# One rotary product in each attention step, output additions behind the keys' low parts, a gate operand in halves, and a shorter look-ahead for the first feed-forward pairs

## The chip, the cores and the metric

The kernel runs on one core of a Trainium2 chip. The metric is the time of one execution in microseconds on the device, lower being better. Five engines take part: TensorE (PE in the profile, with its weight loads as PEld), VectorE (DVE), ScalarE (ACT), GpSimd (POOL) and SyncE (SP), which issues DMAs. Each engine runs its own list of instructions in the order in which the program wrote them, and waits on semaphores for the others.

## The reference

One encoder block on 1024 tokens of width 1024, in float32. What is computed, cut to its core:

```python
h = layer_norm(x, ln0_g, ln0_b)
proj = h @ w_in[l] + b_in[l]
qa, ka, va, qb, kb, vb, ga, gb = jnp.split(proj, IN_SPLITS, axis=-1)
qb = partial_rotary(qb.reshape(B, S, SWA_Q_HEADS, HEAD_DIM), pos)
kb = partial_rotary(kb.reshape(B, S, SWA_KV_HEADS, HEAD_DIM), pos)
y_na = neighbourhood_attention(qa, ka, va, na_rpb[l]) @ w_branch_na[l]
y_swa = windowed_gqa_with_sink(qb, kb, vb, swa_sink[l]) @ w_branch_swa[l]
mixed = jax.nn.sigmoid(ga) * y_na + jax.nn.sigmoid(gb) * y_swa
h = layer_norm(DEEPNORM_ALPHA * h + mixed @ w_out[l] + b_out[l], ln1_g[l], ln1_b[l])
u = jnp.square(jax.nn.relu(h @ w_ff1[l] + b_ff1[l]))
h = layer_norm(DEEPNORM_ALPHA * h + u @ w_ff2[l] + b_ff2[l], ln2_g[l], ln2_b[l])
```

There are eight heads of windowed attention (SWA; 128 tokens to each side, a sink logit per head in the softmax's denominator, two key/value heads) and eight of two-dimensional neighbourhood attention (NA, with a bias table). The rotary turn acts on 16 of the 64 dimensions of SWA's queries and keys.

## The kernel before

**Precision.** Most products are made in three passes from a high and a low part of each operand (high·high, high·low, low·high). So each operand costs a rounding copy, mostly on ACT, and a subtraction, mostly on DVE. `hT` holds the normalised input, transposed; `whi` and `wlo` are the two parts of a weight block, and L278 is the matmul of the projections.

**Stages.** First the layer norm and the first gate products, until about 50 us. Then projections, until about 90. Then 64 attention steps, until about 450: sixteen heads with four steps each, SWA's in steps 0 to 31 and NA's in 32 to 63. Next are the gates (a Strassen scheme over blocks, operands S1 to S3, L851 its matmul, until 545), the branches, the output projection with its layer norm (to 735), the first feed-forward product (FF1, to 1040) and the second (to the end).

**One attention step.** `steps(s)` (L751) writes the parts of different steps in this order:

- `part_a2(s+1)`: DVE adds the sink's share to the sums (L563, SWA alone), takes their reciprocal (L564) and scales the two blocks of exponentials (L567, twice);
- `part_a(s+2)`: PE makes two blocks of scores (L530 and L531). DVE reads each from PSUM, adds the bias and takes the maxima (L533), and then makes the negated maxima (one small instruction, L539 in SWA, L537 in NA);
- a slice of the work that `pump` hands out: the projections of later heads;
- `part_b(s)`: PE transposes the scaled blocks (L588), ACT rounds them (L591), and DVE makes their low parts (L594). `part_e(s+2)`, the exponentials on ACT (L551), is written in the middle of it;
- `flush(False)`, another slice of `pump`, `part_c(s-1)` (PE, L624: the product with the values; in every second step ACT copies one half of it out, L630, and DVE adds the other, L631), `flush`, and the rest of `pump`.

Below, a step is numbered by the count n of L564 on DVE, from 0 at 94.31 us.

**The list `later`.** `defer(0, f, 8, g, ...)` puts functions on a list. Each `flush` runs the entries whose count has come to zero, oldest first, and a number ahead of a function is the count of flushes till it runs. What is deferred is so written behind what is on the list already. Through it go the evacuations of projections:

- `rope` (L385) for SWA's queries and keys: ACT copies the projection out (`qf`, L393), DVE shuffles it (`qs`, L398), POOL makes two products and their sum (L399, L400, L401: 128x512 each), and ACT and DVE make high and low parts (L437, L442). Ten such turns are made, five of them beside attention steps. `rt` holds the cosines and sines.
- `proj_na_qk` (L340) for NA: ACT writes three high parts (L348 to L350), and after `D_NA` flushes DVE makes the low parts `q` and `kl` (L353, L355, L357).
- `turn_v` (L320): ACT's copy and DVE's subtraction for the values `vv` (L326, L327).

**Gates.** `form_hi("S3", g2)` is one ACT copy of a 128x2048 operand into a part of `hT`, `form_lo` one DVE subtraction of that size (L891). `g_sums`, `g_hi` and `g_lo` make a gate's weight operands (L821, L837, L841).

**FF1.** `seq` lists pairs (p, i): block p of the hidden units, product i of seven in a Strassen step. The loop at L1702 runs them: `ff1_mm` on PE (L1313) and `after1` behind it, which evacuates a bank (`act_fn`: DVE L1399 to `usl`). Ahead of each, `prep_to(k)` runs `tick` until k ticks are done. A tick makes the low part of a pair's weights (L1497), the high part of the next pair's (ACT, L1493) and the sums of the pair behind it (L1467, L1482), and asks for later blocks by DMA (`raw`). The larger k is, the more such work is written ahead of the evacuation that follows.

Of the kernel before, what the change touches and what calls it, by code (L numbers as in the profile page):

```python
# [15 lines left out]
P = 128  # L16
# [39 lines left out]
RS = 3, 3.5, 4.5, 5.5  # L56
HI_AT = -1
HI_ACT = (2, 3, 4, 5), ()
ST0=2
# [23 lines left out]
def encoder_block(ctx, tc, x, w_in, w_br, w_out, w_ff1, w_ff2, par, rows, rpbp,  # L83
# [4 lines left out]
    def b32(ap):  # L88
        return ap.bitcast(F32)
# [292 lines left out]

    n_rope = [0]

    def rope(ps, bias, half, then, late=D_ROPE):  # L385
# [9 lines left out]
        def turn():  # L395
            qf = b[0]
            qs = ap.tile([P, 512], F32, tag="vt", name="qs", bufs=1)
            DVE.stream_shuffle(qs, qf, SWAP)  # L398
            POOL.tensor_tensor(out=qf, in0=qf, in1=rt[:, 0, cs], op=ALU.mult)  # L399
            POOL.tensor_tensor(out=qs, in0=qs, in1=rt[:, 1, cs], op=ALU.mult)  # L400
            POOL.tensor_tensor(out=qf, in0=qf, in1=qs, op=ALU.add)  # L401
        hi, lo = then
        defer(0, evac, late[0], turn, late[1], lambda: hi(b[0]), late[2], lambda: lo(b[0]))

# [151 lines left out]
    def part_a2(s):  # L556
# [8 lines left out]
        for i in range(2):  # L565
            p, n, c0 = pns[i]
            DVE.tensor_scalar(out=p[:, :n], in0=p[:, :n], scalar1=st[:, 6 + i:7 + i], scalar2=None, op0=ALU.mult)  # L567

    def part_b(s, between):
# [27 lines left out]
    def part_c(s):  # L597
# [27 lines left out]
        if t % 2 == 1:  # L625

            oo = oT[o_row:o_row + 64, o_chunk, (t // 2) * 512:(t // 2 + 1) * 512]

            def evac():
                ACT.copy(oo, po[64:P, :])  # L630
                DVE.tensor_tensor(out=oo, in0=po[0:64, :], in1=oo, op=ALU.add)  # L631
            if s == 63:
                last_evac.append(evac)
            else:
                evac()

    def fills():
# [29 lines left out]
    with tc.manual_schedule(engines=MANUAL):  # L667
# [116 lines left out]
        def s1_sum(i):  # L784

            DVE.tensor_tensor(out=g1, in0=b32(hT[:, 0, K1, T2]) if i == 0 else g1,
                              in1=b32(hT[:, 0, K2, T2] if i == 0 else hT[:, 1, (K1, K2)[i - 1], T2]), op=ALU.add)
        counts = [CNT[0]] * 8 + [CNT[1]] * 8
        heads_w = []

# [164 lines left out]
        f_add(g2, g1, part("A11", 0), ALU.subtract)  # L955
        last_evac[0]()
        g_hi(2, 1)
# [49 lines left out]
        g_do(3, 5)  # L1007
        form_hi("S3", g2)
        g_sums(2, 7)
        g_sums(3, 7)  # L1010
        g_hi(2, 7)
        form_lo("S3", g2)
        g_lo(2, 7)
# [316 lines left out]
    with tc.manual_schedule(engines=MANUAL):  # L1330
# [371 lines left out]
        for n, (p, i) in enumerate(seq):  # L1702
            prep_to((5, 6, 7)[n] if n < 3 else n + min(LOOK, 5 + n // 3))
            if n == 0:
# [318 lines left out]
```

## Time and profile before

| | us |
|---|---|
| median of 3 runs (lowest to highest) | 1349.87 (1348.58 to 1350.26) |
| the profiled execution's own time | 1348.45 |
| its span | 1346.7 |
| TensorE busy in the span | 1321.3 |
| VectorE busy | 993.5 |
| ScalarE busy | 707.4 |
| GpSimd busy | 278.9 |

The span is the time from the first to the last instruction that the profiler recorded, and 1.75 us lie around it. Matmuls overlap, and their ends are modelled, so a gap that the profile shows on PE is not all that a stop costs: the first matmul behind it has nothing to overlap with. The granted clock of TensorE was 0.998 over the run.

### The profile page before, as it was taken

The page shows a single profiled execution, that of the slowest core. Times are in us where ns is not written, and L with a number is a line of the kernel's source. Part 1 is how long each engine was busy: PE and PEld are TensorE (multiplying, and loading weights), DVE is VectorE, ACT ScalarE, POOL GpSimd, SP SyncE. Part 2 cuts the span into 40 slices and gives each one's busy share as a digit, 9 for nine tenths or more (in the row PEclk, how much of TensorE's full clock was granted, in tenths as well). Part 3 has the DMA queues.
Part 4 walks back from the last instruction along what each step waited for, and adds up shares of the span by engine and source line. Part 5 has one row for each costly group of instructions (what it writes and reads, how often), then busy time and mean ns, then how long its engine had stood idle before and what let it go on. Part 6 is the DMA issues. An engine that isn't in the chain of part 4 may idle for free.

```text
span 1346.7 us, 17318 instructions
## 1 busy us (share of the span) xinstructions
PE 1321.3 (98%) x6296; PEld 1087.7 (81%) x6296; DVE 993.5 (74%) x1617; ACT 707.4 (53%) x1230; POOL 278.9 (21%) x264
## 2 busy tenths in 40 slices
PE   8999999999999999999999999999999999999997
PEld 6788778888888878888888788888888888888785
DVE  7758988877777896443678977677655767787778
ACT  6446666766665545542446755555555533333346
POOL 4351121121120000334630012222100001011207
PEclk9999999999999999999999999999999999999999
DMA  6511111111101332655233566655628644544323
GB/s 230 196 69 48 48 51 41 38 38 44 38 23 39 126 126 103 214 195 198 79 141 133 179 228 203 211 194 181 207 99 304 219 188 149 211 148 176 121 102 125
DMA packets 66422, 183.94 MB, mean 137 GB/s; under 512 B 10400, under 2 KB 12064, under 8 KB 60576
## 3 DMA queue, kind: packets, MB, share of 16 engines
q1 hardware_dynamic: 65904, 182.38, 39.1%
q8 instruction: 49, 0.80, 0.2%
q10 hardware_dynamic: 432, 0.46, 0.1%
q14 instruction: 37, 0.30, 0.1%
HBM read 126.69 MB, written 56.31 MB: 136 GB/s over the span
## 4 chain that ended last, share of the span: by engine, by line
PE 73%; DVE 15%; ACT 7%; issue 2%; POOL 1%; DMA 1%; SPq 0%; DVEq 0%; ACTq 0%; POOLq 0%
PE ps_mm L278 10%; PE ps_mm L1746 6%; PE ps_o L1313 6%; PE ps_s L1746 6%; PE ps_t L1313 6%; PE ps_mm L1313 6%; PE ps_o L1746 5%; PE ps_t L1746 5%; ACT ss L551 3%; DVE ss L567 3%; PE ps_s L1313 2%; DVE ss L533 2%; PE ps_mm L851 1%; PE ps_o L624 1%; PE ps_t L588 1%
## 5 line engine op out<-in xcount | busy, mean ns | idle before, releaser
L278 PE MATMUL ps_mm<-hT,whi 128*128 128x512 f32 x832 | 270.0, 398 | 5.3 <-DVE kl L355 2.6
L278 PEld LDWEIGHTS ps_mm<-hT,whi 128*128 128x128 f32 x832 | 152.9, 188 | 35.3 <-DVE kl L355 4.6
L278 PE MATMUL ps_mm<-hT,wlo 128*128 128x512 f32 x416 | 166.9, 401 | 1.0 <-DVE wlo L684 1.0
L551 ACT ACTIVATE ss<-ss,st 128x384 f32<-128x384 f32 (+1 forms) x128 | 74.5, 585 | 79.9 <-DVE st L539 48.4
L1612 ACT CAST t<-stg 128x2048 fp32r<-128x2048 f32 x28 | 53.4, 1908 | 84.0 <-PE ps_o L1746 47.0
L1765 POOL TENSOR_TENSOR acc<-acc,rst 128x512 f32<-128x512 f32 x16 | 29.5, 1843 | 297.9 <-DMA rst<-xr_d 285.0
L1746 PE MATMUL ps_mm<-t,t 128*128 128x512 f32 x384 | 91.0, 392 | 0.0
L1746 PE MATMUL ps_s<-t,t 128*128 128x512 f32 x384 | 90.8, 392 | 0.0
L278 PEld LDWEIGHTS ps_mm<-hT,wlo 128*128 128x128 f32 x416 | 78.3, 188 | 12.2 <-DVE wlo L684 1.5
L1746 PEld LDWEIGHTS ps_mm<-t,t 128*128 128x128 f32 x384 | 72.1, 188 | 16.3
L1746 PEld LDWEIGHTS ps_s<-t,t 128*128 128x128 f32 x384 | 72.1, 188 | 16.1
L1313 PE MATMUL ps_t<-hS,tw 128*128 128x512 f32 x348 | 84.3, 391 | 0.0
L591 ACT CAST pth<-ps_t 128x384 fp32r<-128x384 f32 (+1 forms) x128 | 51.8, 455 | 52.5 <-PE ps_t L588 51.6
L1313 PEld LDWEIGHTS ps_t<-hS,tw 128*128 128x128 f32 x348 | 65.3, 188 | 14.3
L1615 DVE TENSOR_TENSOR t<-stg,t 128x2048 fp32r<-128x2048 f32 x28 | 65.5, 2338 | 13.1 <-ACT t L1612 13.1
L1135 POOL TENSOR_TENSOR mx<-sg 128x512 f32<-128x512 f32 x16 | 33.5, 2092 | 189.9 <-DVE sg L1134 189.9
L1746 PE MATMUL ps_t<-t,t 128*128 128x512 f32 x288 | 68.6, 392 | 0.4 <-DVE t L1615 0.3
L1746 PE MATMUL ps_o<-t,t 128*128 128x512 f32 x288 | 67.8, 391 | 0.0
L594 DVE TENSOR_TENSOR ptl<-ps_t,pth 128x384 fp32r<-128x384 f32 (+1 forms) x128 | 61.1, 518 | 7.0 <-ACT pth L591 6.8
L1746 PEld LDWEIGHTS ps_t<-t,t 128*128 128x128 f32 x288 | 53.9, 188 | 13.1 <-DVE t L1615 1.3
L1746 PEld LDWEIGHTS ps_o<-t,t 128*128 128x128 f32 x288 | 54.1, 188 | 11.8
L1589 POOL TENSOR_TENSOR rst<-rst,rr 128x512 f32<-128x512 f32 x16 | 22.6, 1412 | 190.7 <-DMA rst<-xn_d 190.7
(306 smaller groups left out, 3170.5 us busy)
## 6 DMA issues: line engine op xcount, KB each, us to landing
us_d<-usl SPq DMA_DIRECT2D x112, 256.0 KB
stg<-us_d SPq DMA_DIRECT2D x28, 1024.0 KB
raw<-in_w_ff SPq DMA_DIRECT2D x36, 512.0 KB
raw<-in_w_in SPq DMA_DIRECT2D x28, 512.0 KB
sg<-sg_d SPq DMA_DIRECT2D x32, 256.0 KB
w2b<-in_w_ff SPq DMA_DIRECT2D x7, 1024.0 KB
w2a<-in_w_ff SPq DMA_DIRECT2D x5, 1024.0 KB
sg_d<-sa SPq DMA_DIRECT2D x16, 256.0 KB
```

Of the source, the lines that this page charges most:

```text
L278: PE.matmul(ps, a[:, k, :], act(b, k), start=(k == 0 and i == 0), stop=(k == NK - 1 and i == 2))
L533: DVE.tensor_tensor_reduce(out=p[:, :n], in0=ps[:, :n], in1=bias_of(j), scale=1.0, scalar=NEG, op0=ALU.add, op1=ALU.max, accum_out=st[:, i ...
L551: ACT.activation(p[:, :n], p[:, :n], AF.Exp, bias=st[:, 2 + i:3 + i], scale=0.125, accum_out=st[:, 4 + i:5 + i])
L567: DVE.tensor_scalar(out=p[:, :n], in0=p[:, :n], scalar1=st[:, 6 + i:7 + i], scalar2=None, op0=ALU.mult)
L591: ACT.copy(pth[:, a:b, :], pv)
L594: DVE.tensor_tensor(out=ptl[:, a:b, :], in0=pv, in1=b32(pth[:, a:b, :]), op=ALU.subtract)
L1135: POOL.tensor_tensor(out=mx[:, f, half * 512:(half + 1) * 512], in0=both[0], in1=both[1], op=ALU.add)
L1313: PE.matmul(ps, ww, act[:, part, k, :], start=(first and k == 0 and m == 0), stop=(k == 3 and m == 2), skip_group_check=True)
L1612: ACT.copy(slot[:, :, 0, :], src)
L1615: DVE.tensor_tensor(out=slot[:, :, 1, :], in0=src, in1=b32(slot[:, :, 0, :]), op=ALU.subtract)
L1746: PE.matmul(ps, st[:, a, part, j * P:(j + 1) * P], w[:, a, wpart, :], start=(first and a == 0 and m == 0), stop=(a == 3 and m == 2), skip_ ...
L1765: POOL.tensor_tensor(out=z, in0=z, in1=t, op=ALU.add)
```

## The change

Four edits.

1. **Rotary products.** Beside attention steps the five operations of `turn` go into a list. The shuffle is run at once if the list was empty. From then on each `part_a2` ends with `rope_step(p)`: POOL copies one column of the block that L567 has just scaled (`junk`, 128x1), and one product is issued behind that copy. With the third product goes the `defer` of the high and low parts, and, if another turn waits in the list, its shuffle, deferred by 8 flushes. Ahead of the attention steps everything is issued at once, as before.
2. **Output additions.** DVE's addition L631 becomes a deferred function of its own (`evac2`), run by the `flush` behind `part_c`, after what is on the list already.
3. **The gate operand S3.** ACT's copy and DVE's subtraction are each made in two halves of 128x1024.
4. **FF1's look-ahead.** The counts for `prep_to` at the first twelve pairs are now a table: 8, 8, 9, 11, 12, 13, 14, 15, 17 at n = 3 to 11, where they were 9, 10, 11, 13, 14, 15, 17, 18, 19. At n = 0 to 2 and from 12 on they are as they were (21 at n = 12).

```diff
+PREP = 5, 6, 7, 8, 8, 9, 11, 12, 13, 14, 15, 17
...
+    in_steps, rope_ops = [], []
+
+    def rope_step(p):
+
+        if rope_ops:
+            j = cp.tile([P, 1], F32, tag="junk", name="junk", bufs=2)
+            POOL.tensor_copy(j, p[:, 0:1])
+            rope_ops.pop(0)()
+            if len(rope_ops) % 5 == 1:
+                rope_ops.pop(0)()
+                if rope_ops:
+                    defer(8, rope_ops.pop(0))
...
-            qs = ap.tile([P, 512], F32, tag="vt", name="qs", bufs=1)
-            DVE.stream_shuffle(qs, qf, SWAP)
-            POOL.tensor_tensor(out=qf, in0=qf, in1=rt[:, 0, cs], op=ALU.mult)
-            POOL.tensor_tensor(out=qs, in0=qs, in1=rt[:, 1, cs], op=ALU.mult)
-            POOL.tensor_tensor(out=qf, in0=qf, in1=qs, op=ALU.add)
+            qs = []
+
+            def shuffle():
+                qs.append(ap.tile([P, 512], F32, tag="vt", name="qs", bufs=1))
+                DVE.stream_shuffle(qs[0], qf, SWAP)
+            ops = [shuffle,
+                   lambda: POOL.tensor_tensor(out=qf, in0=qf, in1=rt[:, 0, cs], op=ALU.mult),
+                   lambda: POOL.tensor_tensor(out=qs[0], in0=qs[0], in1=rt[:, 1, cs], op=ALU.mult),
+                   lambda: POOL.tensor_tensor(out=qf, in0=qf, in1=qs[0], op=ALU.add),
+                   lambda: defer(4 if in_steps else late[1], lambda: hi(qf), late[2], lambda: lo(qf))]
+            if in_steps:
+                rope_ops.extend(ops)
+                if len(rope_ops) == 5:
+                    rope_ops.pop(0)()
+            else:
+                for op in ops:
+                    op()
         hi, lo = then
-        defer(0, evac, late[0], turn, late[1], lambda: hi(b[0]), late[2], lambda: lo(b[0]))
+        defer(0, evac, late[0], turn)
...
             DVE.tensor_scalar(out=p[:, :n], in0=p[:, :n], scalar1=st[:, 6 + i:7 + i], scalar2=None, op0=ALU.mult)
+        rope_step(p)
...
             def evac():
                 ACT.copy(oo, po[64:P, :])
+
+            def evac2():
                 DVE.tensor_tensor(out=oo, in0=po[0:64, :], in1=oo, op=ALU.add)
             if s == 63:
-                last_evac.append(evac)
+                last_evac.extend((evac, evac2))
             else:
                 evac()
+                defer(0, evac2)
...
-        form_hi("S3", g2)
+        for ks in (slice(0, 2), slice(2, 4)):
+            ACT.copy(gop["S3"][:, 0, ks], g2[:, ks])
         g_sums(2, 7)
         g_sums(3, 7)
         g_hi(2, 7)
-        form_lo("S3", g2)
+        for ks in (slice(0, 2), slice(2, 4)):
+            f_add(gop["S3"][:, 1, ks], g2[:, ks], b32(gop["S3"][:, 0, ks]), ALU.subtract)
...
-            prep_to((5, 6, 7)[n] if n < 3 else n + min(LOOK, 5 + n // 3))
+            prep_to(PREP[n] if n < len(PREP) else n + min(LOOK, 5 + n // 3))
```

**The order on the engines.** Matmuls keep their order on PE. On POOL, before, the turns of two projections stand back to back beside the attention steps:

```order
L399 TENSOR_TENSOR qf<-qf,rt 128x512
L400 TENSOR_TENSOR qs<-qs,rt 128x512
L401 TENSOR_TENSOR qf<-qf,qs 128x512
L399 TENSOR_TENSOR qf<-qf,rt 128x512
L400 TENSOR_TENSOR qs<-qs,rt 128x512
L401 TENSOR_TENSOR qf<-qf,qs 128x512
```

and on POOL of the changed kernel the same two turns are (line numbers shift with the edits; L416 to L418 are the products):

```order
L391 COPY junk<-ss 128x1
L416 TENSOR_TENSOR qf<-qf,rt 128x512
L391 COPY junk<-ss 128x1
L417 TENSOR_TENSOR qs<-qs,rt 128x512
L391 COPY junk<-ss 128x1
L418 TENSOR_TENSOR qf<-qf,qs 128x512
L391 COPY junk<-ss 128x1
L416 TENSOR_TENSOR qf<-qf,rt 128x512
```

Each copy stands for one attention step, since it reads what that step's second L567 wrote. The five turns' fifteen products so fall into the steps n = 1 to 3, 7 to 9, 10 to 12, 15 to 17 and 18 to 20. Two turns' shuffles move by one step on DVE (from n = 8 and 16 to 9 and 17, behind the low part of a weight block, L486), and so do the high and low parts that follow them.

On DVE before, in the step n = 31 (the end of SWA's heads; `q` and `kl` are the low parts for NA, `oT` the outputs) stand

```order
L594 TENSOR_TENSOR ptl<-ps_t,pth 128x384 x2
L631 TENSOR_TENSOR oT<-ps_o,oT 64x512
L353 SCALAR_TENSOR_TENSOR q<-ps_mm,prm,q 64x512
L355 SCALAR_TENSOR_TENSOR kl<-ps_mm,prm,kh 64x512
L357 CAST kl<-kl 64x512
L564 RECIPROCAL st<-st 128x2
```

and on DVE of the changed kernel

```order
L620 TENSOR_TENSOR ptl<-ps_t,pth 128x384 x2
L354 SCALAR_TENSOR_TENSOR q<-ps_mm,prm,q 64x512
L356 SCALAR_TENSOR_TENSOR kl<-ps_mm,prm,kh 64x512
L358 CAST kl<-kl 64x512
L659 TENSOR_TENSOR oT<-ps_o,oT 64x512
L589 RECIPROCAL st<-st 128x2
```

The addition moved behind the keys' low parts; the same holds at n = 39, 47 and 55. At n = 23, 25, 33, 41 and 49 it moves behind the subtraction for `vv` (L327) in the same way, and at n = 35, 43 and 51 behind both. In the other steps its place is as before.

On DVE before, at the start of FF1, at the evacuation of pair (0, 7) from the bank `ps_mm`, stand

```order
L1482 TENSOR_TENSOR ts<-raw,ts 128x512
L1497 TENSOR_TENSOR tw_7273<-raw,tw_7273 128x512
L1467 TENSOR_TENSOR ts<-raw 128x512
L1467 TENSOR_TENSOR ts<-raw,ts 128x512
L1497 TENSOR_TENSOR tw_7273<-ts,tw_7273 128x512
L1399 SCALAR_TENSOR_TENSOR usl<-ps_mm,prm,sn 128x512
```

and on DVE of the changed kernel

```order
L1515 TENSOR_TENSOR ts<-raw,ts 128x512
L1432 SCALAR_TENSOR_TENSOR usl<-ps_mm,prm,sn 128x512
L1530 TENSOR_TENSOR tw_7305<-raw,tw_7305 128x512
L1500 TENSOR_TENSOR ts<-raw 128x512
L1500 TENSOR_TENSOR ts<-raw,ts 128x512
```

The evacuation moved ahead of four instructions that prepare weights; these follow it, spread over the next pairs, and at n = 12 four ticks now stand ahead of one pair.

More of the change, by code (lines that the diff above doesn't have):

```diff
@@ L788, in encoder_block @@
         counts = [CNT[0]] * 8 + [CNT[1]] * 8
+        in_steps.append(1)
         heads_w = []
@@ L955, in encoder_block @@
         f_add(g2, g1, part("A11", 0), ALU.subtract)
-        last_evac[0]()
+        for f in last_evac:
+            f()
         g_hi(2, 1)
```

## The prediction

> **What bounds the kernel now.** First the page's head: one engine's share says whether anything else can matter.
>
> ```profile
> span 1346.7 us, 17318 instructions
> PE 1321.3 (98%) x6296; PEld 1087.7 (81%) x6296; DVE 993.5 (74%) x1617; ACT 707.4 (53%) x1230; POOL 278.9 (21%) x264
> ```
>
> PE is busy for 98% of the span, and the change leaves its matmuls and their order alone. So the change can win only out of the 25.4 us (1346.7 − 1321.3) in which PE stands, and what a stop costs beside its gap. Next, the windows view says in which stages it stands (span of the window, then busy time of PE, PEld, DVE, ACT, POOL, each with its count), and the view of waits says for whom (total, times, longest).
>
> ```profile
> 100.00:150.00 50.00, 47.68 (x277) 39.62 (x277) 45.28 (x124) 32.47 (x87) 8.93 (x7) 1.00 0.13 43
> 300.00:350.00 50.00, 49.68 (x285) 42.52 (x284) 38.53 (x101) 31.19 (x72) 9.22 (x17) 1.00 0.14 40
> 450.00:500.00 50.00, 49.10 (x232) 40.08 (x230) 48.26 (x53) 25.85 (x39) 0.00 (x0) 1.00 0.33 118
> 750.00:800.00 50.00, 48.47 (x210) 39.02 (x209) 41.49 (x62) 30.74 (x55) 2.91 (x2) 1.00 0.75 242
> PE ps_s L530 <- DVE st L533: 4.2, 8, 1.0
> PE ps_mm L278 <- DVE kl L355: 2.6, 5, 1.1
> PE ps_mm L1313 <- DVE usl L1399: 1.5, 1, 1.5
> PE ps_o L851 <- DVE hT L891: 0.8, 1, 0.8
> ```
>
> Each edit aims at one of these four waits, together 9.1 us of gaps. All four are waits for DVE, and at 100 us DVE is busy for 45.28 of 50: work there is tight, whatever the mean of 74% says.
>
> **Rotary products: what they cost now.** A turn in the step that begins at 138.94:
>
> ```profile
> 139.11 1.29 POOL L399 TENSOR_TENSOR qf<-qf,rt 128x512 f32<-128x512 f32 x1 [7.02 <-DVE st L564]
> 140.36 1.40 POOL L400 TENSOR_TENSOR qs<-qs,rt 128x512 f32<-128x512 f32 x1
> 139.14 2.84 DVE L567 TENSOR_SCALAR ss<-ss,st 128x384 f32<-128x384 f32 x2
> 146.46 0.75 DVE L567 TENSOR_SCALAR ss<-ss,st 128x384 f32<-128x384 f32 x2
> 98.69 2.57 DVE L567 TENSOR_SCALAR ss<-ss,st 128x384 f32<-128x384 f32 x2
> 142.51 0.44 PE L530 MATMUL ps_s<-kh,q 128*128 128x384 f32 x1 [1.00 <-DVE st L533]
> ```
>
> Two scalings take 0.75 us with POOL idle and 2.84 or 2.57 beside its products: DVE ends with POOL's second product, and PE's next scores start 1.00 late. So a turn costs DVE 1.8 to 2.1 us, five of them some 9.7. What PE loses by it is read from the length of the steps:
>
> ```profile
> 98.49:200.92 102.43, 98.83 (x576) 82.45 (x575) 92.28 (x254) 67.79 (x178) 18.26 (x14) 1.00 0.15 48
> 146.25:165.33 19.08, 18.84 (x113) 16.14 (x111) 17.11 (x51) 14.44 (x38) 0.00 (x0) 1.00 0.26 83
> ```
>
> Four steps without a product take 19.08 us, twenty would take 95.4, and the twenty with the five turns take 102.43. The turns so cost PE **7.0 us**, some 73% of what they cost DVE. That is the most the first edit can win there.
>
> **And after.** The copy that goes ahead of a product waits for the second L567, so the product can't meet this step's scalings. But it must meet something: DVE is busy nine tenths of the time. What follows L567 is L533 twice and then L539. The trace shows both beside a product that ends at 132.09 (130.79 + 1.30), and without one:
>
> ```profile
> 130.79 1.30 POOL L401 TENSOR_TENSOR qf<-qf,qs 128x512 f32<-128x512 f32 x1
> 131.13 0.55 DVE L533 CUSTOM_DVE_ANT_0 ss<-ps_s,bd 128x384 f32<-128x384 f32 x1
> 131.71 0.40 DVE L539 TENSOR_SCALAR st<-st,snk 128x2 f32<-128x2 f32 x1
> 135.28 0.69 DVE L567 TENSOR_SCALAR ss<-ss,st 128x256 f32<-128x256 f32 x2
> 136.35 0.55 DVE L533 CUSTOM_DVE_ANT_0 ss<-ps_s,bd 128x384 f32<-128x384 f32 x1
> 136.95 0.23 DVE L539 TENSOR_SCALAR st<-st,snk 128x2 f32<-128x2 f32 x1
> L162 POOL TENSOR_SCALAR mv<-mv x8: 267/268/355, 638.7 to 720.5; 128x1 f32<-128x1 f32 x8
> ```
>
> L533, which reads PSUM, takes 0.55 in both. L539, which stays in SBUF, takes 0.40 instead of 0.23 and ends 0.02 behind the product: it is held. Undisturbed, the second scaling ends at 135.97 (135.28 + 0.69) and L539 at 137.18, so 1.21 later. In the changed kernel the copy starts when the scaling ends. The trace has no such copy; the nearest rows are POOL's eight instructions on 128x1 (shortest, median and longest in ns): 0.27 as a rule, 0.36 at most. With a product of 1.30 both end 1.57 behind the scaling; with the longest copy, the longest product (1.40) and 0.05 for a semaphore, 1.81. L539 is then held for 0.36 to 0.60, say 0.5, in fifteen steps: 7.5 us of DVE instead of 9.7. By the 73%, PE wins **1.6 us** of its 7.0. I take the middle of the hold; its ends give gains of 3.1 (15 × 0.36 = 5.4 us of DVE) and 0.5 (9.0). The shuffles and low parts that move by a step are the same work; I cost them at nothing, because a step's delay leaves the queries done before the head that uses them, and at up to 0.5 for each of two turns if they pile on the step of L486.
>
> The rule that this step leans on has a page. The Trainium skill, "SBUF — State Buffer", section "SBUF: two separate sides", says that VectorE and GpSimd share one pair of ports as an exclusive lock: the side that starts first keeps it for the whole instruction, and it names VectorE instructions in a fast mode and those with two SBUF inputs. By that rule, the trace agrees: L539 at 0.40 instead of 0.23. The rule speaks against this change, since every product of 1.3 us would catch whatever such instruction comes next; by a rule of free sharing the sum would have the whole 7.0.
>
> **Output additions.** At n = 31 and, alike, at 39, 47 and 55:
>
> ```profile
> 257.20 0.69 ACT L350 ACTIVATE kh<-ps_mm,prm 64x512 fp32r<-64x512 f32 x1
> 258.52 0.68 DVE L631 TENSOR_TENSOR oT<-ps_o,oT 64x512 f32<-64x512 f32 x1 [2.92 <-ACT oT L630]
> 259.98 0.76 DVE L355 SCALAR_TENSOR_TENSOR kl<-ps_mm,prm,kh 64x512 fp32r<-64x512 f32 x1
> 260.79 0.73 PE L278 MATMUL ps_mm<-hT,whi 128*128 128x512 f32 x2 [1.13 <-DVE kl L355]
> 311.03 0.73 PE L278 MATMUL ps_mm<-hT,whi 128*128 128x512 f32 x2 [0.32 <-DVE kl L355]
> ```
>
> DVE stands 2.92 us for ACT's copy L630, adds, and only then frees the bank for which PE waits. With the low parts first, L353 can start in that idle time (ACT's high parts are done at 257.89), and L355 ends by 258.7, some 2 us earlier than now. The bank is then free before PE asks, at 259.66 (260.79 − 1.13). Won: 1.13 once and 0.32 three times, and by the start-to-start distances of the matmuls another 0.28 for each stop (0.17 for an end that is modelled, 0.11 for two matmuls at 0.73 that take 0.62 in a stream): 2.09 + 4 × 0.28 = **3.2 us**. The addition itself is late then; the outputs are first read after 450 us, so nobody waits but DVE's next L564, and DVE has the idle time just named. Of the L355 wait's 2.6 the other 0.5 stands in a step without an addition and stays.
>
> Behind `vv` the same move has nothing to win:
>
> ```profile
> 215.26 0.59 ACT L326 CAST vv<-ps_t 128x512 fp32r<-128x512 f32 x1
> 215.27 0.68 DVE L631 TENSOR_TENSOR oT<-ps_o,oT 64x512 f32<-64x512 f32 x1 [1.71 <-ACT oT L630]
> 215.98 0.69 DVE L327 TENSOR_TENSOR vv<-ps_t,vv 128x512 fp32r<-128x512 f32 x1
> ```
>
> ACT ends at 215.85, so L327 can start 0.13 earlier; the addition, which ran in the wait for ACT, comes behind it and costs DVE about 0.5 (0.68, less 0.13 and what neighbours overlap). In the steps 23 and 25, where DVE is tight, I count 0.4 each on PE by the same 73%: **+0.8**, from 0 (later slack takes it) to 1.2. In NA's steps (33 to 51) PE stands only 0.32 in 50 us, and DVE is idle for more than 11: nothing.
>
> **The gate operand.**
>
> ```profile
> 491.89 2.29 DVE L891 TENSOR_TENSOR hT<-gt,hT 128x2048 fp32r<-128x2048 f32 x1 [0.17 <-ACT hT L897]
> 494.10 0.68 DVE L841 TENSOR_TENSOR gw<-graw,gw 128x512 fp32r<-128x512 f32 x1
> 494.23 8.97 PE L851 MATMUL ps_o<-hT,gw 128*128 128x512 f32 x35 [0.81 <-DVE hT L891]
> ```
>
> With halves PE's second matmul of that product can go after the first, a microsecond earlier. Its third needs the weight's low part from L841, which stands behind both halves and now ends at 494.78; DVE is busy 48.26 of 50 there and saves only the 0.17 for which it waits for ACT's whole copy. So the stop moves by one matmul: **−0.2**, between 0 (a second instruction's own start eats it) and −1.1 (if L841 was not late).
>
> **FF1.**
>
> ```profile
> 753.79 0.68 DVE L1482 TENSOR_TENSOR ts<-raw,ts 128x512 f32<-128x512 f32 x1
> 757.48 0.74 DVE L1399 SCALAR_TENSOR_TENSOR usl<-ps_mm,prm,sn 128x512 f32<-128x512 f32 x1
> 758.28 1.90 PE L1313 MATMUL ps_mm<-hA,tw 128*128 128x512 f32 x7 [1.53 <-DVE usl L1399]
> ```
>
> PE stands from 756.75 for the bank that L1399 empties. In the new order L1399 follows the L1482 of 753.79, so it ends at about 755.2, 1.5 us before PE asks: 1.53 and 0.17 are won. The work that stood ahead isn't gone; n = 12 makes four ticks at once, and blocks are asked for later. I put 0.3 against it, half of one DVE instruction of 0.68 too many ahead of an evacuation (0 to 0.7): **−1.4**.
>
> **Sum.** −1.6 − 3.2 + 0.8 − 0.2 − 1.4 = −5.6. From the profiled execution's 1348.45 (the span and 1.75 around it) that gives 1342.9; this execution lies 1.42 below the median of the runs, 1349.87, so against that median 1344.3.
>
> **The rivals.** *The products are free.* If L539's hold doesn't reach PE (ACT's exponentials wait for L539, and they have idle time), the first edit wins its 7.0, and DVE's spare time also takes the 0.8 at `vv`: −11.8, so 1338.1. For it: L539 is not what PE waits for, only L533 is. Against it: 0.5 us in each of fifteen steps in a stage where DVE has a tenth to spare. Chance 0.24.
>
> *Products are neutral, and the small edits give back.* The five turns cost PE what they did, `vv` costs 1.2, the gate nothing, FF1 gives 0.7 back: −3.2 + 1.2 − 1.0 = −3.0 at best, −2 if the moved low parts cost up to 1: about 1347.4. Chance 0.19.
>
> *Slower: a product that starts later than it must.* If POOL's copy and product start more than some 0.9 us after the scalings (a semaphore, a slow copy), the product's end passes L539, L594's pair and reaches the SBUF instructions behind (L398, L442, L486, or L563 of the next step). Each product then holds DVE for about a microsecond instead of 0.5: 15 us instead of 9.7, which is +3.9 on PE by the 73%, and with −4.0 from the rest that is even. It decides from there on; at a full 1.3 (19.5 us, +7.2) it is +3.2, so 1353. Chance 0.07.
>
> **How the numbers follow.** Forecast 0.50, with a range of its own from 1342 to 1346.5. About 0.2% (2.7 us) is what a measurement can tell from no change, so the border is 1347.2: the forecast, the free products and a third of the neutral case are faster (0.78), the rest of that and the middle of the slow one the same (0.16), 0.06 slower. The range reaches to the free products and past the neutral case, 1337 to 1349.
>
> **What would show it.** Right: no L567 pair over 1 us in steps 1 to 20, L539 near 0.7 in fifteen of them, POOL's products ending 0.02 before it; L278's wait for L355 at 0.5; L1313's for L1399 gone; the first twenty steps at about 100.8 us. Free products would show as about 95.5 there, late ones as a held L594, L442 or L563. The prediction fails if PE finds a new engine to wait for, or if products meet L567 in spite of the copy.

## The result, and the profile after

The changed kernel takes 1336.07 us (median of 4 runs, 1334.97 to 1336.55), the one before 1349.78 in the same measurement: a ratio of 0.9898, 95% interval 0.9882 to 0.9914. It is faster by 13.7 us where 5.6 were forecast, and just below the range. The profiled execution's span fell from 1346.7 to 1334.3 us.

The page's head of the changed kernel, to set beside the two lines of before:

```profile
span 1334.3 us, 17348 instructions
PE 1309.3 (98%) x6296; PEld 1087.4 (81%) x6296; DVE 986.3 (74%) x1618; ACT 707.9 (53%) x1231; POOL 283.5 (21%) x279
```

This is the first thing to see, and it contradicts the prediction's opening. The span lost 12.4 us, but PE's gaps are as long as before: 25.0 us (1334.3 − 1309.3) against 25.4. What became shorter is PE's *busy* time, by 12.0 us, with the same 6296 matmuls in the same order. (A gap is here the span less PE's busy time. A second profile of the changed kernel, further down, has gaps of 22.4 us.)

The waits of PE that the edits were aimed at, in the changed kernel (line numbers are shifted: L555 was L530, L279 was L278, L881 was L851, L1346 was L1313):

```profile
PE ps_s L555 <- DVE st L558: 2.9, 3, 1.6
PE ps_mm L279 <- DVE kl L356: 2.6, 5, 0.8
PE ps_o L881 <- DVE gw L871: 1.0, 1, 1.0
PE ps_o L1346 <- DVE usl L1432: 0.3, 1, 0.3
```

The feed-forward's wait of 1.5 is gone, and one of 0.3 stands at another bank (`ps_o`). The wait for the keys' low parts stands at 2.6 us and five times, as before (1.9 us and five times in the second profile of the same kernel). The gate's stands at 1.0, now for the weight's low part and no longer for the operand. The scores' fell from 4.2 to 2.9, in three stops in place of eight.

Where does the time go, then? Matmuls come in the same order in both kernels, so the n-th matmul can be compared with the n-th. This table gives the time from one to another, worked out from the starts in the traces. `pad64_again` (the kernel before with 64 unused bytes) and `after_again` (the changed kernel) are experiments below; the other columns are the two kernels' own profiles. The two profiles of the changed kernel show how far a row can move by itself: 0.87 us in NA's heads, at most 0.35 in the others.

| from matmul to matmul | before | changed | pad64_again | after_again |
|---|---|---|---|---|
| 400 to 1000: steps 0 to 20, the turns | 108.08 | 105.09 | 107.68 | 105.05 |
| 1000 to 1300: to the end of SWA's heads | 52.95 | 54.86 | 52.83 | 54.91 |
| 1300 to 2400: NA's heads | 195.71 | 194.93 | 195.71 | 194.06 |
| 2400 to 2700: gates | 66.52 | 66.33 | 66.55 | 66.35 |
| 2700 to 3600: branches, output projection | 201.01 | 197.56 | 197.59 | 197.91 |
| 3600 to 3750 | 33.10 | 33.08 | 33.08 | 33.08 |
| 3750 to 3900: FF1's first pairs | 36.46 | 34.87 | 35.96 | 34.83 |
| 3900 to 6200: the rest of FF1, FF2 | 528.42 | 522.77 | 523.09 | 522.82 |
| all | 1222.25 | 1209.49 | 1212.48 | 1209.00 |

The two largest rows, −3.5 and −5.7, lie in stages that none of the four edits touches. There PE has hardly a gap, in either kernel. The windows view of before, for 50 us of the output projection (behind the length: PE's busy time and, in brackets, its matmuls):

```profile
650.00:700.00 50.00, 50.00 (x233) 40.59 (x232) 38.85 (x50) 22.85 (x42) 25.02 (x23) 1.00 0.38 136
```

and that of the changed kernel:

```profile
650.00:700.00 50.00, 50.00 (x242) 41.85 (x241) 39.29 (x53) 23.80 (x46) 22.69 (x21) 1.00 0.37 127
```

PE is busy all the time in both, at a granted clock of 1.00 in both. The windows begin at other places of the program, and PE gets through 9 more matmuls in the second. The single instructions say the same. From the timeline of before (start, duration, line, operands):

```profile
672.02 0.39 PE L1203 MATMUL ps_mm<-wo,m 128*128 128x512 f32 x1
672.25 0.39 PE L1204 MATMUL ps_mm<-wo,m 128*128 128x512 f32 x1
672.48 0.39 PE L1202 MATMUL ps_mm<-wo,m 128*128 128x512 f32 x1
672.72 0.39 PE L1203 MATMUL ps_mm<-wo,m 128*128 128x512 f32 x1
```

and from that of the changed kernel:

```profile
666.50 0.39 PE L1236 MATMUL ps_mm<-wo,m 128*128 128x512 f32 x1
666.72 0.39 PE L1237 MATMUL ps_mm<-wo,m 128*128 128x512 f32 x1
666.95 0.39 PE L1235 MATMUL ps_mm<-wo,m 128*128 128x512 f32 x1
667.18 0.39 PE L1236 MATMUL ps_mm<-wo,m 128*128 128x512 f32 x1
```

The same matmul of 512 columns starts every 0.233 us before (0.70 for three) and every 0.227 after (0.68 for three). That is 6 ns each.

**A first theory.** The one thing in the diff that reaches these stages is `junk`, a tile of one float per partition with two buffers. In the built program each buffer takes 32 bytes of every partition, in the first of the pools that are laid out from the low addresses of SBUF upwards (the left side below; the right side is laid out from the other end). Every tile that is allocated behind it on that side moves by 64 bytes; tiles on the right side stay. In the output projection one operand, `wo`, lies on the left (byte 36,256 of the partition before, 36,320 after), the other, `m`, on the right (212,960 and 221,152). By 256, `wo` has the remainder 160 before and 224 after, and `m` has 224.

### The profile page after: what moved, and what is told of

Same layout as the page of the kernel before. It is cut to its first block, busy times and chain, and to the rows that moved or that the text cites. A ratio compares the mean times of both kernels' runs of the same rounds, so it can differ in the third digit from the quotient of the medians.

```text
span 1334.3 us, 17348 instructions
## 1 busy us (share of the span) xinstructions
PE 1309.3 (98%) x6296; PEld 1087.4 (81%) x6296; DVE 986.3 (74%) x1618; ACT 707.9 (53%) x1231; POOL 283.5 (21%) x279
## 4 chain that ended last, share of the span: by engine, by line
PE 77%; DVE 14%; ACT 5%; issue 1%; POOL 1%; DMA 1%; SPq 0%; DVEq 0%; ACTq 0%; POOLq 0%
PE ps_mm L279 12%; PE ps_mm L1346 7%; PE ps_o L1346 6%; PE ps_mm L1779 6%; PE ps_t L1346 6%; PE ps_s L1779 6%; PE ps_o L1779 5%; PE ps_t L1779 5%; PE ps_s L1346 3%; ACT ss L576 2%; DVE ss L558 2%; PE ps_t L614 2%; PE ps_mm L881 1%; DVE ss L592 1%; PE ps_o L650 1%
## 5 line engine op out<-in xcount | busy, mean ns | idle before, releaser
L279 PE MATMUL ps_mm<-hT,whi 128*128 128x512 f32 x832 | 269.8, 398 | 5.2 <-DVE kl L356 2.6
L279 PEld LDWEIGHTS ps_mm<-hT,whi 128*128 128x128 f32 x832 | 153.0, 188 | 35.0 <-POOL hT L251 3.6
L279 PE MATMUL ps_mm<-hT,wlo 128*128 128x512 f32 x416 | 166.9, 401 | 1.0 <-DVE wlo L713 1.0
L279 PEld LDWEIGHTS ps_mm<-hT,wlo 128*128 128x128 f32 x416 | 78.2, 188 | 12.3 <-DVE wlo L713 1.5
L1346 PE MATMUL ps_t<-hS,tw 128*128 128x512 f32 x348 | 83.6, 389 | 0.0
L1346 PEld LDWEIGHTS ps_t<-hS,tw 128*128 128x128 f32 x348 | 65.3, 188 | 13.6
```

Of the source, the lines that this page charges most:

```text
L279: PE.matmul(ps, a[:, k, :], act(b, k), start=(k == 0 and i == 0), stop=(k == NK - 1 and i == 2))
L1346: PE.matmul(ps, ww, act[:, part, k, :], start=(first and k == 0 and m == 0), stop=(k == 3 and m == 2), skip_group_check=True)
```

## The experiments

Each row is timed beside the kernel before on the same chip. One of pad32's seven executions took 4679.44 us, for a reason that is not known; its median does not rest on it.

| run | median us | ratio to before | 95% interval |
|---|---|---|---|
| pad64 | 1340.11 | 0.9936 | 0.9921 to 0.9950 |
| after_pad64 | 1346.72 | 0.9985 | 0.9976 to 0.9995 |
| pad128 | 1349.82 | 1.0007 | 0.9997 to 1.0016 |
| pad32 | 1353.44 | 1.0034 | 1.0022 to 1.0047 |
| pad192 | 1351.86 | 1.0020 | 1.0010 to 1.0030 |
| pad320 | 1339.41 | 0.9929 | 0.9909 to 0.9949 |
| pad64_again | 1339.43 | 0.9929 | 0.9912 to 0.9945 |
| after_again | 1335.76 | 0.9901 | 0.9886 to 0.9915 |
| rope | 1338.22 | 0.9917 | 0.9903 to 0.9932 |
| oT64 | 1339.03 | 0.9922 | 0.9907 to 0.9937 |
| oT_keys | 1333.88 | 0.9883 | 0.9868 to 0.9897 |
| after_max | 1331.81 | 0.9866 | 0.9850 to 0.9883 |
| early_lo | 1339.63 | 0.9926 | 0.9909 to 0.9942 |
| late_lo | 1339.16 | 0.9923 | 0.9908 to 0.9937 |
| keys_late | 1336.40 | 0.9903 | 0.9888 to 0.9918 |
| keys_max | 1329.07 | 0.9853 | 0.9838 to 0.9867 |

### Is it the place of the tiles, or the edits?

pad64 is the kernel before with an unused tile where the change put its own; after_pad64 the changed kernel with 64 bytes more; pad128 and pad32 are pad64 with other sizes.

```diff
     n_rope = [0]
+    pad = cp.tile([P, 16], F32, name="pad")
+    POOL.memset(pad, 0.0)
```

> The kernel before, with one unused tile of 64 bytes per partition where the change put its junk tile; no other edit. Placement theory (the junk tile moved every later tile of the left pools by 64 bytes, so that the two operands of a matmul have the same remainder by 128 bytes, 96 and 96 in place of 32 and 96): 9 to 11 us faster than before, about 1339.5, the matmuls of the output projection at 227 ns from start to start in place of 233, the gaps of PE as before (25 us). Rival (the four edits brought the 13.7 us): 1349.8, no change, and 233 ns stay.

> The changed kernel with an unused tile of 64 bytes more, so that the left pools' tiles are back at remainder 32 and the four edits stand alone. Placement theory: 9 to 11 us slower than the changed kernel, about 1346.5, so 3 to 4 faster than before. Rival (the edits): 1336, as the changed kernel.

> The kernel before with an unused tile of 128 bytes: every later left tile moves, but its remainder by 128 stays 32. Placement theory: 1349.8, no change, 233 ns in the output projection. Rival (any move of the tiles, or a different order of buffers, does it): about 1339.

> The kernel before with an unused tile of 32 bytes: left tiles at remainder 64, right tiles at 96. If only equal remainders by 128 are fast: 1349 to 1351, matmuls with mixed operands at 229 to 234 ns. If the half of the 128 bytes counts (64 and 96 are both in the upper half): about 1339.5 and 227 ns. If equal remainders by 64 were what counts, before would have been fast (32 and 32), so that is out already.

64 unused bytes alone make the kernel before 8.6 us faster (9.9 in a second measurement). The changed kernel with 64 bytes more, whose tiles no longer agree, takes 1346.7, so its four edits bring 2.0 us against before when they stand alone; set against pad128, whose tiles lie where after_pad64's do, they bring 3.1. 128 bytes change nothing, and 32 make it a little slower. So it is not any move of the tiles, and it is not the edits in the main. The rival fell; of the theory's size (9 to 11) the first measurement fell short by 0.4, and the second lies in it.

The matmuls show it directly. Behind the gates, where PE runs little else than matmuls of 512 columns, the distance from start to start is 226 or 227 ns as a rule in all these kernels where both operands lie on one side. Where one is left and one right, it depends on the run. The medians by line and operands are 226 to 234 ns before (233 or 234 in the output projection), 226 or 227 in pad64, 226 to 234 in pad128 and 232 to 234 in pad32.

### What must agree?

pad32 and pad128 left it open by which number the two places must agree. Before, they agree by 64 and it is slow. I expected 128.

> The kernel before with an unused tile of 192 bytes: left tiles at remainder 96 by 128, as the right tiles, but at 96 by 256 where the right tiles are at 224. If equal remainders by 128 are what counts: as pad64, 8 to 10 us faster than before, 227 ns in the output projection. If by 256 or more: 1349 and 233 ns.

> The kernel before with an unused tile of 320 bytes: left tiles at the right tiles' remainder by 256 (224), but 256 off by 512 (224 against 480). pad192 was slow with equal remainders by 128. If equal remainders by 256 are what counts: as pad64, 8 to 10 us faster than before, 227 ns in the output projection. If by 512 or more: 1349 to 1352 and 233 ns.

pad192 was slow: 1351.86, 0.2% above before. Both sides then stand at 96 by 128, but at 96 and 224 by 256. So the expectation of 128 failed. pad320, which agrees by 256 and not by 512, is as fast as pad64. The windows view of the branches' product (`oS` on the right, weights on the left) for pad64:

```profile
550.00:600.00 50.00, 50.00 (x223) 41.38 (x222) 22.95 (x28) 21.44 (x28) 19.83 (x9) 1.00 0.62 195
```

for pad128:

```profile
550.00:600.00 50.00, 50.00 (x216) 40.06 (x215) 22.43 (x27) 20.31 (x27) 19.81 (x9) 1.00 0.60 191
```

for pad192:

```profile
550.00:600.00 50.00, 50.00 (x216) 40.24 (x215) 22.63 (x27) 20.69 (x27) 19.83 (x9) 1.00 0.60 193
```

and for pad320:

```profile
550.00:600.00 50.00, 50.00 (x222) 41.42 (x221) 22.64 (x27) 21.03 (x27) 19.85 (x9) 1.00 0.63 203
```

The reader is to see 222 or 223 matmuls in 50 us where both operands have the remainder 224 by 256, and 216 where they have not. Of the remainders by 256 tried on the left (32, 96, 160, 192, 224) against 224 on the right, only 224 is fast throughout. 160, that of before, is slow in the output projection and half slow in the branches. Why two operands at different remainders cost some nanoseconds is not shown by these runs.

### How much is left to the edits?

> The kernel before with the unused 64 bytes once more, as the base of after_again: 1340 plus or minus 1.5. The traces' stretches behind the start give 3.0 us between the two; the medians of different chips gave 4 to 5.

> The changed kernel once more, on one chip with the other three. Placement theory: 8.6 of its distance from before are pad64's, and the four edits have the rest, 3 to 5 us below pad64_again.

On one chip, with the operands agreeing in both: 1339.43 and 1335.76, so the edits bring **3.7 us**, and the place of the tiles the other 9.9 of 13.6. The traces give 3.5 (1212.48 − 1209.00 in the table) and 9.8 (1222.25 − 1212.48). The heads of the two pages, pad64_again first:

```profile
span 1337.7 us, 17319 instructions
PE 1311.1 (98%) x6296; PEld 1087.6 (81%) x6296; DVE 992.0 (74%) x1617; ACT 707.4 (53%) x1230; POOL 280.2 (21%) x265
span 1333.1 us, 17348 instructions
PE 1310.7 (98%) x6296; PEld 1088.3 (82%) x6296; DVE 985.3 (74%) x1618; ACT 707.5 (53%) x1231; POOL 283.7 (21%) x279
```

Between these two PE's gaps fall from 26.6 to 22.4 us and its busy time by 0.4. Between the kernel before and pad64_again it is the other way round: the busy time falls by 10.2 (from 1321.3), and the gaps rise by 1.2. So the edits do win out of the gaps, as the prediction had it, and the place of the tiles wins out of the busy time. In the changed kernel's first profile the gaps happened to be 2.6 us longer.

### The turns alone

rope is the first edit alone on the kernel before (its junk tile brings the 64 bytes along).

> The kernel before with the rotary edit alone (its junk tile brings the 64 bytes along, so operands are at equal remainders, as in pad64). The sum on record gave the turns 1.6 us, so 1.6 less than pad64 against the same kernel before, about 1338.5; the trace of the changed kernel suggests about 1 (3.2 won until step 19, some 2 given back in the steps 21 to 25). If the give-back belongs to the additions behind vv and not to the turns: 3 less, about 1337. L564's analogue (negated maxima) held for 0.4 us in fifteen steps either way.

Against pad64_again the traces give 1.7 us in all: 105.42 for matmuls 400 to 1000 (−2.3), 53.58 for 1000 to 1300 (+0.75), and −0.2 over the rest. The median, 1338.22, fits the first expectation (1338.5). So what the additions give back in matmuls 1000 to 1300 of the changed kernel is the rest of its +2.1, about 1.3.

The products do hold an instruction of DVE, as the prediction had it. The timeline of the changed kernel in step 7, with a product that ends at 130.33 (129.04 + 1.29):

```profile
128.15 0.68 DVE L592 TENSOR_SCALAR ss<-ss,st 128x384 f32<-128x384 f32 x2
128.90 0.18 POOL L391 COPY junk<-ss 128x1 f32<-128x1 f32 x1 [17.17 <-DVE ss L592]
129.04 1.29 POOL L416 TENSOR_TENSOR qf<-qf,rt 128x512 f32<-128x512 f32 x1
129.69 0.66 DVE L564 TENSOR_SCALAR st<-st,snk 128x2 f32<-128x2 f32 x1
```

The same kernel's summary of that line over steps 0 to 20 (count, shortest, median and longest in ns, first and last start):

```profile
L564 DVE TENSOR_SCALAR st<-st,snk x21: 228/605/739, 97.0 to 196.3; 128x2 f32<-128x2 f32 x21
```

The scalings (L592) take 0.68 undisturbed. L564, the negated maxima (L539 before; line numbers have shifted, and this is not the L564 by which steps are counted), takes 0.66 in place of 0.23 and ends 0.02 behind the product. By the summary more than half of its 21 runs are held. One by one the trace has fifteen, one for each product, at 0.53 to 0.74 us and 0.64 in the mean.

after_max lets POOL's copy wait for that instruction instead:

```diff
+        rope_step(st[:, 2:3])
         hd.pairs[t] = pns, st
...
-        rope_step(p)
```

(the first place is the end of `part_a`, the second that of `part_a2`.)

> The changed kernel with one edit: POOL's copy ahead of a product waits for the negated maxima (the instruction that the products held) in place of the second scaling, so a product starts about 1 us later. Hold theory (0.4 us of DVE in fifteen steps, of which PE loses 73% at most): the maxima are back at 0.23 us in all fifteen, and up to 4 us are won, about 1333, as long as nothing else is held. Rival (the hold costs PE nothing): no change. Second rival: the product now holds what follows, L442's or L486's analogue or the scalings of the next step, by 0.4 us or more, and the time is the same or 1 to 3 more.

The same summary of after_max:

```profile
L564 DVE TENSOR_SCALAR st<-st,snk x22: 228/229/230, 96.9 to 197.0; 128x2 f32<-128x2 f32 x22
```

All are back at 0.23, and the time is 1331.81, 4.0 to 4.3 below the changed kernel's two medians (3.5 by the trace, against after_again's). The second rival appears in part: in three of the fifteen steps the product now holds the weights' low part (1.9 us in place of 1.2), in two the queries' (1.1 in place of 0.7), and it still pays. So the hold did cost PE time, and the sum is this: the fifteen holds were 15 × 0.41 us (0.64 − 0.23), 6.2 us of DVE; the new ones are 3 × 0.7 + 2 × 0.4 = 2.9. DVE is freed of 3.3 us, and PE is 3.5 to 4.3 faster. PE so gained about what DVE was freed of; what all fifteen holds cost PE can't be read from this run.

### The additions

oT64 is the second edit alone on pad64. oT_keys is the changed kernel with the additions deferred in four steps only:

```diff
-                defer(0, evac2)
+                if s in (29, 37, 45, 53):
+                    defer(0, evac2)
+                else:
+                    evac2()
```

> The kernel before with the 64 unused bytes and the additions' edit alone. By the sum on record: 2.4 less than pad64 (3.2 at the keys, 0.8 given back behind vv). By the changed kernel's trace: the stops at n = 31, 39, 47 and 55 gone, new ones at 37, 45 and 53 in their place, so 0.5 to 1 less than pad64. If the stops at 37, 45 and 53 come only because the turns put PE ahead, they don't appear here.

> The changed kernel with the output additions deferred only in the four steps where they go behind the keys' low parts alone (n = 31, 39, 47, 55); behind vv, and behind vv and keys, they stand as before. If the new stops at n = 37, 45 and 53 come from the additions behind vv and keys (n = 35, 43, 51): they go, and the time is 2 to 3 less than the changed kernel, with 0.8 of it from the steps 23 and 25. If they come from PE being early there: they stay, 0 to 0.8 less.

oT64 needs 54.54 us for matmuls 1000 to 1300 (+1.7, the additions behind `vv`) and 194.23 for 1300 to 2400 (−1.5). The two cancel: by the median the edit alone brings 0.4 us against pad64_again (1339.03 and 1339.43), by the trace nothing (0.9 more), where the sum on record had 2.4. The stop in step 37 is in it too (0.51 us), so it doesn't come from the turns. In oT_keys the four useful places alone give 192.72 for 1300 to 2400: −3.0. The wait for `kl` falls to 0.5 in one stop, and the time to 1333.88, 1.9 to 2.2 below the changed kernel. So the new stops come from the additions moved in NA's steps, behind `vv` alone (33, 41, 49) or behind both `vv` and the keys (35, 43, 51). Which of the two, the traces say. DVE in oT_keys in step 35, where the addition stands ahead of `vv`:

```profile
280.72 0.68 DVE L659 TENSOR_TENSOR oT<-ps_o,oT 64x512 f32<-64x512 f32 x1 [1.75 <-ACT oT L656]
281.33 0.69 DVE L328 TENSOR_TENSOR vv<-ps_t,vv 128x512 fp32r<-128x512 f32 x1
```

and the changed kernel's timeline, DVE and then PE:

```profile
281.84 0.69 DVE L328 TENSOR_TENSOR vv<-ps_t,vv 128x512 fp32r<-128x512 f32 x1 [2.37 <-ACT vv L327]
282.56 0.74 DVE L354 SCALAR_TENSOR_TENSOR q<-ps_mm,prm,q 64x512 fp32r<-64x512 f32 x1
284.89 0.68 DVE L659 TENSOR_TENSOR oT<-ps_o,oT 64x512 f32<-64x512 f32 x1
292.98 0.76 DVE L356 SCALAR_TENSOR_TENSOR kl<-ps_mm,prm,kh 64x512 fp32r<-64x512 f32 x1
293.88 0.70 PE L279 MATMUL ps_mm<-hT,whi 128*128 128x512 f32 x2 [0.75 <-DVE kl L356]
```

In both DVE still stands ahead of `vv`, so what the addition of step 33 delayed is caught up there. But in the changed kernel the addition of step 35 runs last in its step, at 284.89, and not in that wait. DVE so enters the next steps later, and two steps on, at 293.74, it is late with the next keys' low part. A wait of the same name took the place of the one removed.

### The moved low parts

After step 13 and after step 21 the changed kernel stops PE for longer than before. The changed kernel's timeline of step 13, DVE and PE behind it:

```profile
161.30 1.22 DVE L511 TENSOR_TENSOR wlo<-raw,whi 128x1024 fp32r<-128x1024 f32 x1
162.55 1.39 DVE L467 TENSOR_TENSOR q<-qf,q 64x512 fp32r<-64x512 f32 x2
166.21 0.39 PE L555 MATMUL ps_s<-kh,q 128*128 128x256 f32 x1 [1.15 <-DVE st L558]
```

The queries' low parts (L467) stand behind the weights' (L511) there. My theory was that these steps had become too long. early_lo puts those of turns 7 and 9 back to steps 12 and 20 (with the high parts that go ahead of them), late_lo puts them to 14 and 22:

```diff
-                   lambda: defer(4 if in_steps else late[1], lambda: hi(qf), late[2], lambda: lo(qf))]
+                   lambda: defer((1 if half and n_rope[0] > 6 else 4) if in_steps else late[1], lambda: hi(qf), late[2], lambda: lo(qf))]
```

```diff
+                   lambda: defer(4 if in_steps else late[1], lambda: hi(qf),
+                                 14 if half and n_rope[0] > 6 else late[2], lambda: lo(qf))]
```

> The changed kernel with one edit: the queries' low parts of the turns 7 and 9 go back to the steps 12 and 20, where they stood before, in place of 13 and 21 behind the weights' low part. Pile theory (these two steps became too long for DVE, and so give back what the turns won): PE's stops of 1.15 us in step 14 and 1.56 in step 22 shrink below 0.5, 1.5 to 2.5 us less than the changed kernel. Rival (the held instruction of 0.4 us in each product step adds up): no change of more than 0.5.

> The changed kernel with one edit: the queries' low parts of the turns 7 and 9 stand one step later than in the changed kernel, in the short steps 14 and 22, no longer behind the weights' low part of 13 and 21. Pile theory: the stops of 1.15 us (step 14) and 1.56 (step 22) go or shrink below 0.4, and 1.5 to 2.5 us are won against the changed kernel, about 1334. Rival (the holds of 0.4 us in the product steps add up to these stops): they stay above 1 us, and the time moves by less than 0.5.

Both came out 3 to 4 us *slower* than the changed kernel, which neither expectation held. The timeline of early_lo:

```profile
158.56 1.39 DVE L467 TENSOR_TENSOR q<-qf,q 64x512 fp32r<-64x512 f32 x2 [2.23 <-ACT q L462]
161.63 0.44 PE L555 MATMUL ps_s<-kh,q 128*128 128x384 f32 x1 [2.04 <-DVE st L558]
```

and of late_lo:

```profile
210.12 0.38 PE L556 MATMUL ps_s<-kh,q 128*128 128x256 f32 x1 [3.54 <-DVE q L468]
```

Earlier, DVE stands 2.23 us for ACT's high part (L462). That needs the third product of the same step, which ends at 155.51, and ACT makes it from 157.91 on, behind that step's exponentials and the weights' high part. Later, PE waits for the low part itself. So neither of the two steps tried is better for them, and whether the length of step 13 alone makes the stop can't be told from these two. after_max says more: with the holds gone the stop behind step 13 falls from 1.15 to 0.45 us, that behind step 21 only from 1.56 to 1.32. The holds were part of the first; what makes the second stays open.

> Both mendings on the changed kernel: additions deferred only behind the keys' low parts (as in oT_keys), and the queries' low parts one step later (as in late_lo). If the two effects add: about 4 less than the changed kernel, 1331 to 1332.5. If the steps 21 to 25 share one cause: no more than 2.5 less, as oT_keys alone.

keys_late (oT_keys with late_lo) takes 1336.40: about late_lo's loss and oT_keys' gain against the changed kernel (3.1 and 2.2) together, and neither 4 nor 2.5 less, since late_lo is no mending.

### The best of them

> The changed kernel with the additions deferred only behind the keys' low parts (oT_keys) and POOL's copy waiting for the negated maxima (after_max). If the two effects are apart: 4.0 and 3.2 us by the traces, so about 7 less than the changed kernel, 1329. If the first is a wait that hides the second: no better than after_max, 1331.8.

keys_max has after_max's edit and oT_keys' on the changed kernel. The head of its page:

```profile
span 1326.9 us, 17341 instructions
PE 1307.2 (99%) x6296; PEld 1089.1 (82%) x6296; DVE 984.1 (74%) x1618; ACT 708.2 (53%) x1231; POOL 281.6 (21%) x279
```

and its wait for the keys' low parts, one of PE's waits:

```profile
PE ps_mm L279 <- DVE kl L356: 0.5, 1, 0.5
```

1329.07 us: the two gains are apart and add, as expected (1329). It beats the changed kernel by 6.7 us on the same chip and the one before by 20.3 (ratio 0.9853, 0.9838 to 0.9867). PE's gaps are down to 19.7 us.

## Why the prediction was wrong

**The step that failed** stands in the first paragraph: "PE is busy for 98% of the span, and the change leaves its matmuls and their order alone. So the change can win only out of the 25.4 us in which PE stands". The order listing showed the matmuls in the same order, and I took the same order for the same time. But busy time is not fixed by the list of instructions. It fell by 12.0 us, and the gaps by 0.4. pad64 and pad64_again show that 64 bytes of an unused tile bring 8.6 to 9.9 us without any edit; that is what carried the time below the range. The listing did show the tile (`junk`, 128x1), and I asked only what its copy takes, not where its memory lies and what it moves.

**The rival that the time points to is not what happened.** "The products are free" gave 1338.1, near the measured 1336.07, and rested on L539's hold costing PE nothing. The hold is there (0.64 us in the mean of fifteen in place of 0.23), and after_max, which removes it, is 3.5 to 4.3 us faster. A time near a rival's is no evidence for it; the row that the prediction named for it (about 95.5 us for the first twenty steps) spoke against it: they took 99.59 (99.02 to 198.61).

**The edits by themselves** bring 3.7 us where the sum had 5.6. Term by term, by the traces and against pad64_again (together −3.4 to −3.0 of the 3.5 that the traces give):

| term | forecast | measured | by |
|---|---|---|---|
| turns | −1.6 | −1.7 | rope |
| additions behind the keys' low parts | −3.2 | −3.0 | oT_keys |
| additions behind `vv` | +0.8 | +1.3 to +1.7 | after_again less rope; oT64 |
| additions in NA's steps behind `vv`, or `vv` and keys | 0 | +1.3 | after_again less oT_keys |
| gate operand | −0.2 | −0.2 | after_again |
| FF1 | −1.4 | −1.1 | after_again |

- *Turns: right in mechanism; that −1.7 falls on −1.6 is in part luck.* The scalings are undisturbed, and what takes the collision's place is a hold of 0.41 us (0.36 to 0.60 on record, 0.5 taken). The copy is 0.18 us, shorter than the 128x1 rows that I had (0.27). The sign named for it, the maxima near 0.7 in fifteen steps, shows as 0.64 in fifteen. The first twenty steps took 99.59 us where the sign was 100.8, and 0.75 is given back behind them. By the 73%, 15 × 0.41 = 6.2 us of DVE would have given 2.6. So about one us is missing against that, and two errors cancel. Two stops behind the steps 13 and 21 are where it can have gone; the moved low parts stand there, which I had costed "at nothing", at 0.5 each at most. PE in rope, at both places:

```profile
166.85 0.38 PE L555 MATMUL ps_s<-kh,q 128*128 128x256 f32 x1 [1.15 <-DVE st L558]
207.86 0.39 PE L555 MATMUL ps_s<-kh,q 128*128 128x256 f32 x1 [1.53 <-DVE st L558]
```

and in pad64_again, where only the second of them is a stop:

```profile
209.21 0.39 PE L532 MATMUL ps_s<-kh,q 128*128 128x256 f32 x1 [0.68 <-DVE st L535]
```

So the two grow by 1.15 and 0.85. A part of that is the holds': in after_max the stops are 0.45 and 1.32, so they have grown by 0.45 and 0.64. No run shows whether that rest comes of the low parts' place.

- *The rule of the Trainium skill* ("SBUF — State Buffer", section "SBUF: two separate sides") that one side keeps the shared ports for the whole instruction: the trace agrees. L564 ends 0.02 us behind the product, and takes 0.23 where the product starts behind it.
- *Keys: right where the additions stand behind them alone.* The low parts came a little later than the working had them: at n = 31 DVE starts them at 257.76, when ACT's last high part is done, and ends L356 at 259.28 and not by 258.7. That is early enough, and PE has no stop there. The failed part is the sentence "In NA's steps (33 to 51) PE stands only 0.32 in 50 us, and DVE is idle for more than 11: nothing." DVE's idle time there is in waits of its own, and an addition that used one of them was moved out of it. So the wait for `kl` came back in the steps 37, 45 and 53. This is the rule that the prediction applied at `vv`, and didn't apply ten steps later.
- *`vv`: right in sign, too small.* 0.8 was put, 1.2 at most; the runs have 1.3 to 1.7.
- *Gate: right.* PE now does the second matmul early and stops for the weight's low part ahead of the third, as the prediction had it. The changed kernel's timeline of DVE and PE:

```profile
490.71 2.36 DVE L921 TENSOR_TENSOR hT<-gt,hT 128x1024 fp32r<-128x1024 f32 x2
492.98 0.69 DVE L871 TENSOR_TENSOR gw<-graw,gw 128x512 fp32r<-128x512 f32 x1
493.72 3.48 PE L881 MATMUL ps_o<-hT,gw 128*128 128x512 f32 x14 [1.03 <-DVE gw L871]
```

- *FF1: right.* The wait of 1.53 is gone, and a smaller one comes at the place where four ticks stand together; with what stands around it, it gives back 0.6 where 0.3 was put. The changed kernel's timeline:

```profile
773.34 0.74 DVE L1432 SCALAR_TENSOR_TENSOR usl<-ps_o,prm,sn 128x512 f32<-128x512 f32 x1
774.14 3.03 PE L1346 MATMUL ps_o<-hA,tw 128*128 128x512 f32 x12 [0.28 <-DVE usl L1432]
```

## What to carry to other kernels

When a span is nearly all PE, watch the distance between the starts of like matmuls, not only the gaps: here some 6 ns of 233 in matmuls with mixed operands are worth more than four edits to the order. A new tile, however small, can move every tile allocated behind it, so a change that adds one is to be measured against the old kernel with the same number of unused bytes. Moving an instruction behind another is free only if the idle time that it ran in before is not the only idle time that its engine has nearby.

## What the runs showed of the hardware that was not expected

Where PE runs little else than fp32r matmuls of 512 columns (behind the gates), the distance between their starts is 226 to 227 ns as a rule where the two operands' start bytes have the same remainder by 256 (seen with both at 32, 96, 160, 192 and 224), and mostly 229 to 234 ns where they differ (left 32, 96, 160 or 192, right 224); agreement by 128 isn't enough (pad192, 1351.86 us), and disagreement by 512 does no harm (pad320, 1339.41 us). In this kernel the difference is 9.9 us of 1349. It is not the only thing that sets the distance: beside the attention steps, where other matmuls stand between them, the projections' matmuls take 224 to 236 ns in pad64 too, where both operands have 224. The cause inside the chip is not shown. A POOL copy of 128x1 that waits for DVE takes 0.18 us here, and the product behind it starts 0.14 us after the copy's start.
